# Hybrid encoder layer: token forms one iteration sooner, additions that free a PSUM bank first, final norms in two interleaved parts

## The chip, the cores and the metric

The kernel runs on one core of one Trainium2 chip, in one launch. The metric is the device time of one execution in microseconds (us), lower is better; the time before is the median of three runs. The profile is of one execution, and all times of day in it are counted from the start of its span.

## The reference

One encoder layer over 1024 tokens of width 1024, in float32, then a final norm:

```python
h = h + hybrid_mixer(rms_norm(h, ln_mix_g), ...)      # RG-LRU group and attention group, then y @ w_o
h = h + conv_glu_ffn(rms_norm(h, ln_ffn_g), w_up, conv_w, conv_b, w_down)
return rms_norm(h, final_norm_g)

def rms_norm(x, g):
    return x * lax.rsqrt(mean(x * x, axis=-1) + 1e-6) * g
def conv_glu_ffn(xn, w_up, w, b, w_down):
    u = depthwise_conv(xn @ w_up, w, b, 1)            # three taps along the tokens
    g, val = u[..., :2816], u[..., 2816:]
    return (silu(g) * val) @ w_down
```

## The kernel before, in words

Everything is float32, and each matrix product is made of three TensorE passes: an operand is split into a high part (ScalarE writes the copy rounded to fp32r) and a low part (VectorE or GpSimd subtracts the high part from the source), and high x high, high x low and low x high are added up in one PSUM bank. `split` (lines 57 to 67) does that; line 62 is its ScalarE copy, line 67 its subtraction.

After the attention the rest of the program is in hand-written order: inside `manual_schedule` each engine and the DMA queue (SP) execute in the order of the program text. `order.close()` ends one such block and the next one begins; at that seam the build's planner merges the two orders, so that a few instructions of the second block can stand before the last ones of the first. A pool's PSUM bank or SBUF slot that is given out again makes its next writer wait until all its readers are done.

The output projection is a loop over the 8 token tiles `i` (128 tokens each). Iteration `i` transposes the attention half of tile `i+1` (`mla_in`), multiplies (`mix`, 24 matmuls), adds to `hh[i]`, stores `hh[i]` to DRAM (`hs`), turns an earlier tile's normalised rows into the token forms that the next stage needs (`tr2`: four transposes per form, then a split), and normalises `hh[i]` in place (`norm2`, line 937 its last multiplication). The four banks of `oneC` go round: each transposed or projected block takes the next one.

The feed-forward products use a two-level scheme with seven products for eight (Strassen-Winograd): forms B11, B21, B22 and the sums T1 to T4 of the token side (`sums_a`, `sums_b` lines 953 to 961, `tr_sum`), and for each of the 22 column pairs `j` four forms of the up-projection weights (`W[0..3, j]`, made by `combine`, lines 972 to 977, and `split`). `prod(n, j, ps, new)` is 12 matmuls into one bank. `spare` hands out, in turn, banks that the pair loop doesn't use yet, for the transposes of the forms; the order in which forms take spare banks decides which bank waits for which split.

The pair loop (line 1321 on) runs seven products for pair `j`, and beside them on ScalarE and VectorE: the convolution taps of the gate (`glu_gate`) and of the value (`glu_value`, with the Silu of line 1192) of this and the pair before, the product of the two (`glu_out`, which spills the seven forms for the down projection to DRAM), the weight forms of pair `j+1` (`prep0`, `prep_sums`), and the additions between products (`add`, line 1083). One of them, `add(vh, vl, ts_)`, reads the bank `vl` that product 4 then writes on, so product 4 waits for it. In the last pair, `look_ahead` fetches and makes the first operands of the down projection.

The down projection is a loop over `todo`: 7 passes `p` of 11 blocks `q`, 12 matmuls each, in four banks `x` or `y`. `make(n)` builds a block's operands four blocks ahead: it splits a spilled form (`A` part) and a form of the down weights (`W` part); for some passes VectorE first forms a sum of weights. The last four blocks of pass 6 stand apart (`LAST`), ordered by token tile: all four blocks of tile `j`, then the addition to `hh[4+j]`, then its final norm. `norm3` squares a row tile on ScalarE with a running sum, takes the root, gets the reciprocal root on VectorE in five [128,1] operations (lines 83 to 87), multiplies by the gain (line 1276) and stores. In pass 6 the norms of tiles 0 to 3 stand between the makes.

## Time and profile before

| | us |
|---|---|
| median of 3 runs (lowest, highest) | 1245.88 (1244.98, 1251.24) |
| the profiled execution | 1245.23 |
| its span, first to last instruction | 1243.3 |
| TensorE matmul busy | 1174.3 (94%) |
| TensorE weight load busy | 974.5 (78%) |
| VectorE busy | 939.1 (76%) |
| ScalarE busy | 642.8 (52%) |
| GpSimd busy | 268.2 (22%) |
| mean granted TensorE clock | 0.977 |

The span is the time from the first to the last instruction of the profiled execution; 1.93 us of the execution lie outside it. PE is TensorE (PEld its weight loads), DVE VectorE, ACT ScalarE, POOL GpSimd, SP the queue that issues DMAs. The profile divides the chain of work that ended last as 77% PE, 14% DVE, 4% issue, 3% ACT and 2% DMA. A timeline row is start, duration, engine, line, operation, output<-inputs, shapes and count; in brackets stand the idle time of the engine before it and what ended that.

### The profile page before, as it was taken

To read this page: it belongs to the slowest core of one execution; us is meant where nothing else is said; L and a number is where in the kernel's file an instruction comes from. 1 tells how busy PE (TensorE), PEld (TensorE's weight loads), DVE (VectorE), ACT (ScalarE), POOL (GpSimd) and SP (SyncE) were. 2 spreads that over 40 slices of the span, in tenths; PEclk is the share of its full clock that TensorE was granted. 3 is DMA by queue.
4 is the path that set the end of the run, shared out by engine and by line. 5 is a ranking of instruction groups with operands and counts; after the bars stand their busy time and mean duration, and the time that the engine had idled before them with its cause. 6 is when DMAs were issued, how large, how long until landed. Compare 5 with 4: busy or idle time off the path is not lost.

```text
span 1243.3 us, 15331 instructions
## 1 busy us (share of the span) xinstructions
PE 1174.3 (94%) x5668; PEld 974.5 (78%) x5668; DVE 939.1 (76%) x1374; ACT 642.8 (52%) x1029; POOL 268.2 (22%) x150
## 2 busy tenths in 40 slices
PE   6998887999999999998799999999999989999994
PEld 5976765788888888787688888888888878888873
DVE  6788789777777755586778787787877867787675
ACT  5645466676777763343544445444454445344442
POOL 2224456631212433353101011010110000000000
PEclk9999998999999999999899999999999999999997
DMA  6311110000000142230333322333223179653222
GB/s 210 101 43 43 34 35 17 18 1 1 1 1 1 51 154 85 85 111 8 93 110 103 122 96 79 108 104 122 91 84 108 53 258 348 207 178 105 98 94 84
DMA packets 93578, 113.37 MB, mean 91 GB/s; under 512 B 5184, under 2 KB 59840, under 8 KB 93504
## 3 DMA queue, kind: packets, MB, share of 16 engines
q1 hardware_dynamic: 93504, 112.40, 27.3%
q8 instruction: 44, 0.72, 0.2%
q14 instruction: 30, 0.25, 0.1%
HBM read 82.76 MB, written 28.57 MB: 90 GB/s over the span
## 4 chain that ended last, share of the span: by engine, by line
PE 77%; DVE 14%; issue 4%; ACT 3%; DMA 2%; SPq 0%; POOL 0%; DVEq 0%; ACTq 0%; POOLq 0%
PE vl L1080 18%; PE x L1269 7%; PE y L1269 7%; PE pt L763 4%; PE p L1080 4%; PE gh L1080 4%; PE gl L1080 4%; PE av L774 3%; PE av L773 3%; PE sc L70 2%; PE sc L71 2%; PE sc L72 2%; DVE bc L223 1%; PE pso L71 1%; PE pso L72 1%
## 5 line engine op out<-in xcount | busy, mean ns | idle before, releaser
L1080 PE MATMUL vl<-T,w 128*128 128x512 f32 x792 | 198.7, 400 | 10.1 <-DVE vh L1083 10.1
L1080 PEld LDWEIGHTS vl<-T,w 128*128 128x128 f32 x792 | 150.7, 191 | 46.9 <-DVE vh L1083 11.3
L67 POOL TENSOR_TENSOR w<-rg,w 128x1024 fp32r<-128x1024 f32 x21 | 52.0, 2478 | 356.8 <-ACT w L62 220.2
L749 DVE TENSOR_REDUCE nm<-sc 128x1 f32<-128x1024 f32 x64 | 78.2, 1221 | 30.3 <-PE sc L72 30.0
L62 ACT ACTIVATE ptb<-pt 128x512 fp32r<-128x512 f32 x128 | 70.2, 596 | 58.7 <-PE pt L763 57.6
L67 DVE TENSOR_TENSOR ptb<-pt,ptb 128x512 fp32r<-128x512 f32 x128 | 82.9, 680 | 7.0 <-ACT ptb L62 7.0
L756 ACT ACTIVATE pr<-sc,nm 128x1024 f32<-128x1024 f32 x64 | 71.7, 1120 | 2.3 <-DVE nm L749 2.3
L763 PE MATMUL pt<-ident,pr 128*128 128x128 f32 x512 | 67.6, 274 | 3.3 <-DVE ptb L67 3.3
L763 PEld LDWEIGHTS pt<-ident,pr 128*128 128x128 f32 x512 | 59.3, 140 | 14.1 <-DVE ptb L67 5.4
L773 PE MATMUL av<-ptb,vt 128*128 128x256 f32 x256 | 66.1, 295 | 0.0
L1173 ACT ACTIVATE c<-gh,vv 128x512 f32<-128x512 f32 x22 | 17.1, 779 | 92.0 <-DVE gh L1083 92.0
L1080 PE MATMUL gh<-B,w 128*128 128x512 f32 x264 | 64.3, 392 | 0.0
L774 PE MATMUL av<-ptb,vt 128*128 128x256 f32 x256 | 63.9, 286 | 0.0
L1080 PE MATMUL p<-T,w 128*128 128x512 f32 x252 | 62.5, 397 | 0.0
L1269 PE MATMUL x<-abS 128*128 128x512 f32 x264 | 60.2, 389 | 0.0
L1269 PE MATMUL y<-abS 128*128 128x512 f32 x264 | 60.2, 389 | 0.0
L1080 PEld LDWEIGHTS gh<-B,w 128*128 128x128 f32 x264 | 49.5, 188 | 11.4
L1080 PE MATMUL vl<-B,w 128*128 128x512 f32 x240 | 58.4, 392 | 0.0
L1080 PE MATMUL gl<-B,w 128*128 128x512 f32 x240 | 57.6, 389 | 0.0
L1269 PEld LDWEIGHTS x<-abS 128*128 128x128 f32 x264 | 49.6, 188 | 10.3
L1269 PEld LDWEIGHTS y<-abS 128*128 128x128 f32 x264 | 49.6, 188 | 10.3
L1080 PEld LDWEIGHTS p<-T,w 128*128 128x128 f32 x252 | 47.4, 188 | 11.4
(638 smaller groups left out, 2979.9 us busy)
## 6 DMA issues: line engine op xcount, KB each, us to landing
rg<-in_wup SPq DMA_DIRECT2D x22, 512.0 KB, 4.1
rv<-in_wup SPq DMA_DIRECT2D x22, 512.0 KB, 3.8
S<-c SPq DMA_DIRECT2D x44, 256.0 KB, 2.6
wr<-in_wdn SPq DMA_DIRECT2D x44, 256.0 KB, 5.4
stS<-S SPq DMA_DIRECT2D x44, 256.0 KB, 2.9
A<-c SPq DMA_DIRECT2D x33, 256.0 KB, 2.1
stA<-A SPq DMA_DIRECT2D x33, 256.0 KB, 5.2
wost<-in_wo SPq DMA_DIRECT2D x8, 512.0 KB, 3.7
```

Source lines behind the costliest of these rows:

```text
L62: act.activation(hi, src, AF.Copy)
L67: (dve if lo_on == "dve" else pool).tensor_tensor(out=lo, in0=src, in1=hi.bitcast(F32), op=ALU.subtract)
L70: pe.matmul(ps, l[0], r[0], start=start, stop=False)
L71: pe.matmul(ps, l[0], r[1], start=False, stop=False)
L72: pe.matmul(ps, l[1], r[0], start=False, stop=stop)
L749: dve.reduce_max(nm[t], sc[t], axis=AX, negate=True)
L756: act.activation(pr[t], sc[t], AF.Exp, bias=nm[t], accum_out=rowsum[:, h, i:i + 1])
L763: pe.transpose(pt[:, ts(c, P)], pr[t][:, ts(4 * kh + c, P)], ident)
L773: pe.matmul(av[:, 0:256], lv, ptb[buf][:, 0, c, :], start=(c == 0), stop=False)
L774: pe.matmul(av[:, 0:256], lv, ptb[buf][:, 1, c, :], start=False, stop=(c == NT - 1))
L1080: pe.matmul(ps, w[:, l, ko + k, :], b[:, r, k, :], start=a_, stop=z_, skip_group_check=True)
L1269: pe.matmul(ps, ab[:, 0, l, ts(j, P)], ab[:, 1, r, :], start=a_, stop=z_, skip_group_check=True)
```

## The change

The token forms of tile `i-1`, and not `i-2`, are made in iteration `i` of the output projection, and the sums with them; the sums of tile 7 go from GpSimd to VectorE and stand between the first form transposes, of which T2 comes first. The sums of pair 1's weights are formed in the scratch `c0`, earlier. In pairs 0, 1 and the last, the addition that product 4 waits for stands before (last pair: between) the operand work that it followed, and the first weight form of pair 2 and the first two fetches of the down operands move to the start of an iteration. In the down projection a sum of weights (b21 + b11) is formed one pass sooner. The squares of the right half of tiles 4 to 7 are summed during pass 6, and in the last four tiles the VectorE part of a norm stands one tile later than its ScalarE part.

```diff
         for i in range(NT):
...
-            if i >= 2:
-                tr2(i - 2, oneC)
+            if i >= 1:
+                tr2(i - 1, oneC)
             norm2(i)
-            if i >= 6:
-                sums_b(i - 2, pool)
+            if i >= 5:
+                sums_b(i - 1, pool)
             if 4 <= i < NT - 1:
                 sums_a(i, pool)
...
-        tr2(6, spare)
-        sums_b(6, pool)
-        sums_a(7, pool)
...
     c0 = stp.tile([P, S], F32, tag="st", name="c0")
+    tr_sum("T2", 0, spare)
     prod(1, 0, VL[0], True)
-    tr_sum("T2", 0, spare)
+    sums_a(7, dve)
     tr_sum("T2", 1, spare)
+    tr_sum("T2", 2, spare)
+    split(W[0, 1][:, 0], W[0, 1][:, 1], raw[1][0], "act", "dve")
     copy(c0[:, lo], VL[0])
-    split(W[0, 1][:, 0], W[0, 1][:, 1], raw[1][0], "act", "dve")
     prod(2, 0, GL, True)
-    tr_sum("T2", 2, spare)
     tr2(7, spare)
-    sums_b(7, pool)
+    sums_b(7, dve)
     add(GL, GL, c0[:, lo])
     spares.remove(S1)
     prod(1, 1, VL[1], True)
     tr_sum("T2", 3, spare)
+    s3 = c0[:, lo].rearrange("p (k n) -> p k n", k=4)
+    combine(1, s3, dve)
     prod(2, 1, S1, True)
...
-    def prep_sums(j, between=None, zs=(3, 2, 1)):
+    def prep_sums(j, between=None, zs=(3, 2, 1), s3=None):
         rg, rv = raw[j]
-        s3 = fw.tile([P, 4, P], F32, tag="s3", name=f"s3{j}")
-        combine(j, s3, dve)
+        if s3 is None:
+            s3 = fw.tile([P, 4, P], F32, tag="s3", name=f"s3{j}")
+            combine(j, s3, dve)
...
-        if bf == "T4":
-            dve.tensor_tensor(out=b21, in0=b21, in1=b11, op=ALU.add)
         split(ab[:, 1, 0], ab[:, 1, 1], src, "act", "dve")
         if bf == "B21":
             dve.tensor_tensor(out=b11, in0=b12, in1=b11, op=ALU.subtract)
+        if bf == "B22":
+            dve.tensor_tensor(out=b21, in0=b21, in1=b11, op=ALU.add)
...
-    def norm3(i):
-        junk = fw.tile([P, D], F32, tag="w3", bufs=2, name=f"jf{i}")
-        act.activation(junk, hh[i], AF.Square, accum_out=ss_f[:, i:i + 1])
-        r = rsqrt(ss_f[:, i:i + 1], 1, 1.0 / D, f"rf{i}")
+    def norm3_half(i):
+        junk = fw.tile([P, 512], F32, tag="w3", bufs=2, name=f"jg{i}")
+        act.activation(junk, hh[i][:, hi], AF.Square, accum_out=ss_f[:, i:i + 1])
+        for k, m in ((0, 1.0), (1, -0.5)):
+            dve.tensor_scalar(out=part[:, k, i:i + 1], in0=ss_f[:, i:i + 1], scalar1=m / D, scalar2=m * EPS, op0=ALU.mult, op1=ALU.add)
+
+    def norm3_act(i, part_only=False):
+        junk = fw.tile([P, 512 if part_only else D], F32, tag="w3", bufs=2, name=f"jf{i}")
+        act.activation(junk, hh[i][:, lo] if part_only else hh[i], AF.Square, accum_out=ss_f[:, i:i + 1])
+        return rsqrt_act(ss_f[:, i:i + 1], 1, 1.0 / D, f"rf{i}", part[:, 0, i:i + 1] if part_only else None)
+
+    def norm3_dve(i, sq, part_only=False):
+        r = rsqrt_dve(sq, ss_f[:, i:i + 1], 1, 1.0 / D, f"rf{i}", part[:, 1, i:i + 1] if part_only else -0.5 * EPS)
...
     fetch_raw(2, 0)
     prod(7, 0, VL[0], False)
-    prep_sums(1, None, (2, 1, 3))
     ts_ = aside(T1, 0)
     add(VH[0], VL[0], ts_)
     prod(3, 0, GH, True)
+    gh = GH
+
+    def first_gh():
+        add(gh, gh, c0[:, hi])
+        add(gh, gh, ts_)
+
+    prep_sums(1, None, (1, 2), s3)
+    first_gh()
+    split(W[3, 1][:, 0], W[3, 1][:, 1], s3, "act", "dve")
     cgs[0] = conv_start(0, GL)
-    add(GH, GH, c0[:, hi])
-    add(GH, GH, ts_)
     prod(4, 0, VL[0], False)
...
-        if 1 < j < NPAIR - 1:
+        if j < NPAIR - 1:
             prep0(j + 1)
+        else:
+            fetch_to(2)
...
-        if j == 1:
-            prep0(2)
-        else:
+        if j > 1:
             prod(2, j, C11[j], False)
...
         prod(7, j, vl, False)
-        if not last:
+        if j == 1:
+            add(vh, vl, ts_)
+            prep_sums(2)
+        elif not last:
             prep_sums(j + 1, lambda: add(vh, vl, ts_))
         else:
-            look_ahead()
+            fetch_to(8)
+            make(0)
+            make(1)
             add(vh, vl, ts_)
+            make(2)
+            make(3)
...
+    part = f2.tile([P, 2, NT], F32, name="part")
...
         if p == 6 and q < 4:
-            norm3(q)
+            norm3_dve(q, norm3_act(q))
+            norm3_half(4 + q)
+    sqs = {}
     for j in range(4):
         for q in range(NQ - LAST, NQ):
             down(xs[j], j, ready[len(todo) - NQ + q], False, q == NQ - 1)
         into(1, 0, xs, j)
-        norm3(4 + j)
+        sqs[j] = norm3_act(4 + j, True)
+        if j:
+            norm3_dve(3 + j, sqs[j - 1], True)
+    norm3_dve(7, sqs[3], True)
```

## Rows read from the trace of the kernel before

**Rows 1.** Who waited for whom, PE alone: us in total, times, longest us.
```profile
PE vl L1080 <- DVE vh L1083: 10.1, 3, 4.2
PE x L1269 <- ACT res L62: 6.1, 4, 3.9
```
**Rows 2.** Busy time by stretch; after the engines PEclk, DMA share, GB/s.
```profile
614.00:982.00 368.00, 367.97 (x1584) 298.71 (x1585) 292.57 (x381) 174.33 (x228) 46.29 (x19) 1.00 0.32 103
596.80:600.20 3.40, 3.40 (x10) 2.63 (x9) 2.52 (x4) 0.78 (x1) 0.00 (x0) 0.50 0.97 278
613.90:617.30 3.40, 3.27 (x8) 2.60 (x9) 2.55 (x4) 1.56 (x2) 0.00 (x0) 0.50 0.64 186
1008.00:1012.00 4.00, 4.00 (x17) 3.28 (x18) 3.93 (x7) 1.99 (x4) 0.00 (x0) 1.00 0.62 230
```
**Rows 3.** Timeline of PE, forms and first pairs, in order.
```profile
567.84 2.38 PE L1080 MATMUL vl<-B,wo 128*128 128x512 f32 x9 [2.33 <-DVE wo L67]
...
580.34 3.06 PE L1080 MATMUL t<-T,w 128*128 128x512 f32 x12 [0.70 <-DVE T L67]
...
595.93 7.35 PE L1080 MATMUL vl<-T,w 128*128 128x512 f32 x24 [4.25 <-DVE vh L1083]
...
614.03 4.54 PE L1080 MATMUL vl<-T,w 128*128 128x512 f32 x12 [2.38 <-DVE vh L1083]
...
623.97 2.24 PE L1080 MATMUL vl<-T,w 128*128 128x512 f32 x9
```
**Rows 4.** Timelines of DVE and POOL at the end of the projection.
```profile
552.85 1.10 DVE L85 TENSOR_TENSOR rh6t<-rh6r 128x1 f32<-128x1 f32 x1
...
562.04 2.29 DVE L937 SCALAR_TENSOR_TENSOR h<-h,rh7r,g 128x1024 f32<-128x1024 f32 x1
...
566.04 1.74 DVE L67 TENSOR_TENSOR wo<-rg,wo 128x1024 fp32r<-128x1024 f32 x1
...
552.62 1.31 POOL L960 TENSOR_TENSOR h<-h,h 128x512 f32<-128x512 f32 x1
```
**Rows 5.** Groups by line and shape, 586 to 640 us.
```profile
L67 DVE TENSOR_TENSOR w<-rv,w 128x1024 fp32r<-128x1024 f32 x3 | 3.7, 1217 | 0.0
...
L1192 ACT ACTIVATE c<-c 128x1024 f32<-128x1024 f32 x3 | 3.2, 1061 | 0.3 <-DVE c L1178 0.3
...
L1173 ACT ACTIVATE c<-gh,vv 128x512 f32<-128x512 f32 x3 | 2.3, 778 | 8.4 <-DVE gh L1083 8.4
...
L1178 DVE SCALAR_TENSOR_TENSOR c<-gh,vv,c 128x512 f32<-128x512 f32 x3 | 2.3, 751 | 0.1
...
L976 DVE TENSOR_TENSOR rg<-rv,rg 128x512 f32<-128x512 f32 x3 | 2.1, 692 | 2.7 <-POOL w L67 2.5
```
**Rows 6.** Timelines of PE and DVE, last pair.
```profile
1008.00 3.06 PE L1080 MATMUL vl<-T,w 128*128 128x512 f32 x12 [3.46 <-DVE vh L1083]
...
1002.55 0.69 DVE L67 TENSOR_TENSOR abA<-wr,abA 128x512 fp32r<-128x512 f32 x1
```
**Rows 7.** Timelines of PE and DVE, last pass and tail.
```profile
1190.44 19.20 PE L1269 MATMUL x<-abA 128*128 128x512 f32 x84
...
1203.20 0.68 DVE L67 TENSOR_TENSOR abA<-stA,abA 128x512 fp32r<-128x512 f32 x1
...
1206.23 0.15 DVE L83 TENSOR_SCALAR rf2xh<-ss_f 128x1 f32<-128x1 f32 x1 [0.35 <-ACT jf L1273]
...
1207.34 1.28 DVE L1276 SCALAR_TENSOR_TENSOR hf<-hf,rf2r,g 128x1024 f32<-128x1024 f32 x1
1208.54 0.68 DVE L67 TENSOR_TENSOR res<-stA,res 128x512 fp32r<-128x512 f32 x1
...
1227.25 0.68 DVE L1083 TENSOR_TENSOR hf<-x,hf 128x512 f32<-128x512 f32 x1
...
1231.46 0.68 DVE L1083 TENSOR_TENSOR hf<-x,hf 128x512 f32<-128x512 f32 x1
...
1238.67 1.42 DVE L1276 SCALAR_TENSOR_TENSOR hf<-hf,rf7r,g 128x512 f32<-128x512 f32 x2
```

More of the change, by code (lines that the diff above doesn't have):

```diff
@@ L1301, in make @@
             ready[n] = operands(*ORDER[p], q, home)
-    def look_ahead():
-        fetch_to(6)
-        for n in range(4):
-            make(n)
     fetch_raw(2, 0)
     prod(7, 0, VL[0], False)
-    prep_sums(1, None, (2, 1, 3))
     ts_ = aside(T1, 0)
```

## The prediction

> **What bounds the kernel now.** I read the waits of PE first, then busy time by stretch, then the timelines where PE stands still. From 614 to 982 us PE is busy 367.97 of 368 us at a granted clock of 1.00 [rows 2]: nothing that this change does to ScalarE, VectorE or the queues can shorten that stretch. What can be won lies where PE waits. Of those waits two kinds are touched here: 10.1 us in three waits for the addition that frees the bank `vl`, and 6.1 us for the split operands `res` of the last pass [rows 1]. The reader should see that the three bank waits are 4.25, 2.38 and 3.46 us [rows 3, 6], and that two of them cost more than themselves: after 595.93 and after 614.03 there are 3.4 us at a granted clock of 0.50, that is 1.2 instead of 2.4 GHz [rows 2], where 1.7 us of work each is lost. After the 3.46 us wait the clock stayed at 1.00 [rows 2]. The third place is the tail, where no engine is busy: the additions of two neighbouring row tiles start 4.21 us apart (1231.46 less 1227.25), and the last multiplication ends at 1238.67 + 1.42 = 1240.1 [rows 7].
>
> **The own time.** The sum is made against the profiled execution, 1245.23 us, of which 1243.3 are span; the median of the runs is 0.65 higher, less than I can resolve, so no correction is made.
>
> **Part one, the tail and the last pass.** Before, each block of pass 6 with a norm behind it takes 1208.54 - 1203.20 = 5.34 us on VectorE [rows 7], since it goes low part, sum of weights, ScalarE copy, low part, norm, one after the other. The sum of weights goes to the pass before, where VectorE then has three operations of 0.7 us for 12 matmuls of PE (2.7 us), so it is hidden there; without that cover it would cost 11 x 0.7 = 7.7 us. The new step has two low parts of 0.68, five small operations that last at most 1207.34 - 1206.23 = 1.11, the multiplication with 1.20 to the next start, and two new [128,1] operations. These are not in the trace; between 0.15 (a small one) and 0.35 more for a wait as before the same row, I take 0.2 each [rows 7]. Sum 4.07; overlapped starts take some 0.15 off: 3.9. PE begins pass 6 at 1190.44 and passes 84 matmuls in 19.2 us, 0.227 each [rows 7]. VectorE is done with the `y` additions 0.9 later, at 1191.3, so the last of the seven remaining blocks is ready at 1191.3 + 4 x 3.9 + 3 x 1.3 = 1210.8. PE wants it after 93 matmuls, at 1211.5. So PE doesn't stop; the margin is 0.7, and the point from which it stops is a step of 4.1 us.
>
> The half squares are new on ScalarE: 512 columns with a running sum, between a 512-column copy with scale (0.78) and a 1024-column one (1.06) [rows 5]; I take 0.8 with its read-out. ScalarE's step is then two copies, a whole square, a root and a half square, about 3.2 us, under VectorE's 3.9, so it is hidden; if not, it has 0.7 to go.
>
> Row tile 4 is then complete at 1190.44 + 96 x 0.227 + 0.2 = 1212.4, tile 7 at 1220.6. VectorE's order is add 4, add 5, norm 4, add 6, norm 5, add 7, norm 6, norm 7; a norm is five small operations back to back (1.0) and 1.2, and its root was taken on ScalarE meanwhile. Add 5 starts at 1215.2 (12 matmuls after tile 4): 0.7 and 2.2 give 1218.1; add 6 and norm 5, 2.85, give 1220.9; add 7 and norm 6 give 1223.75; norm 7 has 1.0 and two halves of together 1.42 and ends at 1226.2. Against 1240.1 that is **13.9 us less**; what follows, the last stores, is the same. The price ends are 8.8 (PE stops as today, see the second rival) and 14.6 (every small operation at 0.15).
>
> **Part two, the last pair.** PE is ready for product 4 at 1008.00 - 3.46 = 1004.54. VectorE's second block, the last work now ahead of the addition, ended at 1002.55 + 0.69 = 1003.24 even with the fetches as late as they were [rows 6]; the addition takes 0.7, so it is done at 1003.95 and nothing waits. The two blocks that go behind it are wanted by PE 5 us and more later. The early fetches stand in SP's queue ahead of one spill and wait for the slot of form B11, which product 1 of this pair lets go; all else in the queue has its old order. **3.4 us less**; at worst the fetch order costs the same again (0).
>
> **Part three, forms and first pairs.** I follow them to one point, product 6 of pair 2, which started at 623.97 [rows 3] and after which PE doesn't wait.
>
> In the projection loop the number of form transposes stays; tile `i-1` is normalised before PE ends the multiplication of tile `i`, so they find their rows ready. At its end VectorE sets the pace. Row 552.85 shows a [128,1] product that took 1.10 us while a GpSimd sum ran from 552.62 on for 1.31, and the multiplication of tile 7 took 2.29 where the same shape takes 1.28 at rest [rows 4, 7]: such operations wait for GpSimd's. The two sums taken from GpSimd let the last multiplication run at rest (1.0 less) and the split of pair 1's weights take 1.22 instead of 1.74 [rows 4, 5]; the same two pairs of sums cost VectorE 4 x 0.69 [rows 5], half of it ahead of that split. With 0.4 us from PE's four transposes that left the loop's end, product 1 of pair 1 starts 0.5 sooner than 567.84. Against that, one form fewer takes a spare bank, so all later forms move on by one, and the bank that product 5 wants (0.70 wait at 580.34 [rows 3]) is freed one split of 0.6 later. The four operations of `combine` (2.8 us) move into VectorE's gaps there. Net 0, between 1.8 sooner (a row tile's whole contention) and 1.7 later.
>
> The Trainium skill, "SBUF — State Buffer", section "Who interferes with whom", has it that a VectorE instruction with two SBUF inputs and a GpSimd instruction that reads SBUF exclude each other for a whole instruction. By that rule the sums that the change pulls forward keep GpSimd busy under the last two norms, which speaks against a gain here; without it the tile would be ready 1.8 sooner. The contended row agrees with the rule, and I go by it.
>
> Product 3 of pair 0 ended at 595.93 - 4.25 = 591.7 [rows 3] and now ends at 592.0. From there two chains race. PE: products 4 | 6, 5, 7, 3, 4 of pair 1 | 1, 5 of pair 2, eight of 2.77 = 22.2. VectorE, from the addition to `VH` at 589.2 on: 0.7, two weight splits 2.4, two additions 1.3, a split 0.6, a wait of 0.25 on ScalarE's tap (0.78), eight taps of 0.75, the gate product 1.2: 601.7, where it waits for product 7 of pair 1. PE's product 7 itself waits 0.2 for the copy behind the Silu and ends at 592.0 + 4 x 2.77 + 0.2 = 603.3. Then addition 0.65, `combine` 2.8, three splits 3.1, addition 0.7, ScalarE's tap 0.85, four taps 3.0: 614.4; the Silu 1.06 and a copy 0.6: 616.1 [rows 5]. PE arrives at product 6 at 592.0 + 22.2 + 0.2 = 614.4 and waits 1.7. So the 10 us of waits and slow clock (4.25 + 2.38 + 3.4) become one new wait of 1.7: 623.97 - 616.1 = 7.9 less. The first weight form of pair 2 now stands ahead of the value's taps on ScalarE; its copy needs columns whose fetch waits in SP for a slot that the first of the two weight splits frees, at 591.1. The value's taps on VectorE begin at 597.6, behind a copy (1.06) and a tap (0.78), so the fetch has 4.7 us to land; each us more holds up taps, Silu and product 7 by one. At the seam of the two blocks the planner may put the last form's transposes behind product 7; its bank is then what product 3 waits for, 0.8 later. I take **7.2 us less**, with 3.7 and 9.6 as ends.
>
> **Sum.** 13.9 + 3.4 + 7.2 = 24.5; 1245.23 - 24.5 = 1220.7.
>
> **The rivals.**
> First: the first pairs give it back. PE now waits about 3 us ahead of product 1 of pair 1 (it arrives sooner, the split hardly) and 1.7 ahead of product 6. A 2.38 us wait was followed by the half clock and 3.46 was not [rows 2, 3, 6], so either may cost 1.7. Both, and the seam's 0.8: 7.2 becomes 3.0, time 1224.9. The Trainium skill, "TensorE: Matmul & The Clock Gate", section "HAM oscillation — how this bites in real kernels", has gaps between matmul groups send the clock to half so that the next group starts cold; by that rule alone this rival would be the rule, and the trace bears it out in two of the three bank waits.
> Second: the operand chain stays the bound of pass 6. If the step stays 5.34, the last block is ready at 1191.3 + 21.4 + 3.9 = 1216.6, 5.1 late: time 1225.8. For it: 5.34 is what is measured. Against: two of its links are gone by the text.
> Third: the additions don't come sooner, because merging at the seam or a fetch that blocks SP holds VectorE up as before. Then only the tail remains, 1245.23 - 13.9 = 1231.3. For it: three queues meet there. Against: order inside a block is that of the text.
> Fourth, slower: in the attention only PE's order is written by hand; the rest is the planner's, over 59 steps. If it orders VectorE otherwise and a step loses over 24.5 / 59 = 0.42 us, the gain is gone; at 0.6 the time is 1256. Against: nothing changes ahead of the projection loop.
>
> **How the numbers follow.** Forecast 0.66 (own range 1217.5 to 1223.5), first rival 0.16, second 0.07, third 0.04, fourth 0.04, better than 1217 (no new wait, all upper ends) 0.03. The range of 1217 to 1228 leaves out the last three of these, 0.11, and the far edges of the others. A change of 0.5%, 6.2 us, is what a measurement of this kernel tells from none; faster by more than that are all cases but the fourth (part of it is the same): faster 0.95, same 0.02, slower 0.03.
>
> **What would show it.** PE without a wait for `vh` at all; no idle PE in pass 6 and a clock of 1.00 to its end; row additions in the tail 2.85 apart; the last multiplication ending 14 us after tile 4's last matmul; one wait near product 6 of pair 2 of about 1.7 us. It is wrong if PE waits on `res`, if half-clock stretches follow 567 or 614, or if the stretch to 500 us has another length.

## The result, and the profile after

The changed kernel takes 1227.36 us (median of 4 runs, 1227.13 to 1228.26), the kernel before 1247.36 beside it (4 runs, 1244.98 to 1251.24): a ratio of 0.9838 [0.981, 0.9866], 20 us faster (17 to 24). The forecast was 1220.7, range 1217 to 1228; the time lies in the range by 0.6 us, and above the 1217.5 to 1223.5 that the forecast gave as its own. The profiled execution took 1227.5 us with a span of 1225.7; the comparison below is made between the two spans, 1243.3 and 1225.7.

Who waited for whom, PE alone, after: us in total, times, longest. The three waits for the bank `vl` and those for `res` [rows 1] are gone; what stands there now are waits for split forms, weights and normalised rows.

```profile
PE pshB L942 <- DVE h L937: 3.8, 3, 1.6
...
PE vl L1076 <- DVE wo L67: 2.6, 1, 2.6
PE vl L1076 <- ACT gl L1082: 1.5, 1, 1.5
PE gh L1076 <- DVE T L67: 1.4, 1, 1.4
PE t L1076 <- DVE T L67: 1.3, 1, 1.3
```

Timeline of PE after, in order of time: where these waits fall. The first three are in the projection loop, where PE transposes a tile that has just been normalised; the rest answer to [rows 3], and the last two lines to the head of [rows 7].

```profile
525.21 1.17 PE L942 MATMUL pshB<-ident,h 128*128 128x128 f32 x8 [1.58 <-DVE h L937]
...
553.67 0.63 PE L942 MATMUL pshB<-ident,h 128*128 128x128 f32 x4 [0.88 <-DVE h L937]
...
561.27 0.65 PE L942 MATMUL pshB<-ident,h 128*128 128x128 f32 x4 [1.36 <-DVE h L937]
...
572.35 3.85 PE L1076 MATMUL vl<-B,wo 128*128 128x512 f32 x10 [2.58 <-DVE wo L67]
576.70 3.05 PE L1076 MATMUL s<-B,wo 128*128 128x512 f32 x12
...
586.86 3.06 PE L1076 MATMUL t<-T,w 128*128 128x512 f32 x12 [1.29 <-DVE T L67]
...
596.91 3.02 PE L1076 MATMUL gh<-B,w 128*128 128x512 f32 x12 [1.41 <-DVE T L67]
...
624.50 1.88 PE L1076 MATMUL vl<-T,w 128*128 128x512 f32 x7 [1.50 <-ACT gl L1082]
...
1187.38 18.98 PE L1269 MATMUL x<-abA 128*128 128x512 f32 x83
...
1206.42 11.04 PE L1269 MATMUL x<-res 128*128 128x512 f32 x48
```

Busy time by stretch, after (columns as in [rows 2]): one stretch at the half clock is left in this part, behind the wait at 572.35; the last pass runs at full clock to its end.

```profile
573.50:576.90 3.40, 3.40 (x12) 2.71 (x11) 1.30 (x2) 0.00 (x0) 0.00 (x0) 0.53 0.02 5
614.00:982.00 368.00, 366.50 (x1584) 297.23 (x1583) 294.86 (x385) 176.38 (x231) 46.24 (x19) 1.00 0.32 103
1187.00:1217.50 30.50, 30.46 (x135) 24.89 (x133) 23.62 (x64) 17.76 (x42) 0.00 (x0) 1.00 0.25 95
```

To see where the time went I cut each profile at five points of PE's timeline, the same instructions in every kernel. A runs from the first transposes of the projection's second loop (`psyt`, tile 0) to the start of product 2 of pair 1 (into `s`); B from there to product 3 of pair 0 (into `gh`); C to product 6 of pair 2 (the point of part three); "rest" to the start of the last pass; D to the end of the span. All are differences of start times in the profiled executions, us:

| kernel | run median | psyt at | A | B | C | A+B+C | rest | D |
|---|---|---|---|---|---|---|---|---|
| before | 1247.36 | 502.32 | 68.46 | 17.88 | 35.31 | 121.65 | 566.47 | 52.86 |
| after | 1227.36 | 503.91 | 72.79 | 20.21 | 27.59 | 120.59 | 562.88 | 38.32 |
| tail_only | 1235.86 | 504.98 | 69.48 | 18.33 | 36.59 | 124.40 | 569.42 | 38.30 |
| forms_back | 1224.92 | 503.90 | 70.71 | 17.96 | 29.46 | 118.13 | 562.90 | 38.37 |
| one_turn_on | 1225.84 | 504.72 | 71.00 | 17.96 | 28.62 | 117.58 | 562.90 | 38.30 |
| pairs_back | 1229.28 | 504.27 | 72.10 | 20.70 | 30.60 | 123.40 | 562.79 | 38.34 |
| norms_whole | 1230.91 | 503.53 | 71.24 | 20.21 | 27.83 | 119.28 | 562.86 | 42.23 |
| t4_late | 1239.32 | 502.73 | 71.21 | 20.21 | 27.79 | 119.21 | 562.89 | 51.17 |
| copy_first | 1223.00 | 503.95 | 71.47 | 17.96 | 26.74 | 116.17 | 564.40 | 38.28 |
| sums_late | 1223.01 | 502.38 | 70.38 | 17.96 | 28.66 | 117.00 | 562.89 | 38.33 |
| copy_first2 | 1223.74 | 503.05 | 69.81 | 17.98 | 25.17 | 112.96 | 564.32 | 38.27 |
| w01_first | 1224.18 | 504.08 | 68.67 | 20.19 | 28.20 | 117.06 | 562.86 | 38.30 |
| combined | 1221.64 | 504.59 | 69.99 | 17.94 | 25.16 | 113.09 | 564.20 | 38.32 |
| three_moves | 1221.05 | 505.35 | 66.98 | 19.75 | 25.16 | 111.89 | 564.19 | 38.27 |

Before to after: 14.5 from D, 3.6 from "rest", 1.1 from A to C, and 1.6 lost ahead of `psyt`: 17.6, the difference of the spans. Code ahead of `psyt` is the same in all fourteen kernels, and its start lies anywhere from 502.3 to 505.4; so I compare kernels by A to D and "rest", which leave that out, and by the medians. The four kernels with 564.2 to 564.4 in "rest" have a wait of 1.15 to 1.28 us there, at product 4 of pair 2.

### The profile page after: what moved, and what is told of

The parts are those of the page before. It is cut to its first block, busy times and chain, and to the rows that moved or that the text cites. A ratio compares the mean times of both kernels' runs of the same rounds, so it can differ in the third digit from the quotient of the medians.

```text
span 1225.7 us, 15357 instructions
## 1 busy us (share of the span) xinstructions
PE 1167.1 (95%) x5668; PEld 970.8 (79%) x5668; DVE 939.6 (77%) x1386; ACT 641.3 (52%) x1037; POOL 260.2 (21%) x146
## 4 chain that ended last, share of the span: by engine, by line
PE 81%; DVE 12%; ACT 2%; DMA 2%; issue 2%; SPq 0%; DVEq 0%; POOL 0%; ACTq 0%
PE vl L1076 19%; PE x L1269 9%; PE y L1269 7%; PE gh L1076 5%; PE gl L1076 4%; PE pt L763 4%; PE p L1076 4%; PE av L774 3%; PE av L773 2%; PE sc L70 2%; PE sc L71 2%; PE sc L72 2%; DVE bc L223 1%; PE pso L71 1%; PE pso L72 1%
## 5 line engine op out<-in xcount | busy, mean ns | idle before, releaser
L1076 PE MATMUL vl<-T,w 128*128 128x512 f32 x792 | 195.7, 396 | 2.0 <-ACT gl L1082 1.5
L773 PE MATMUL av<-ptb,vt 128*128 128x256 f32 x256 | 64.9, 292 | 0.0
L774 PE MATMUL av<-ptb,vt 128*128 128x256 f32 x256 | 62.6, 283 | 0.0
```

The lines of the kernel that those rows point to most:

```text
L773: pe.matmul(av[:, 0:256], lv, ptb[buf][:, 0, c, :], start=(c == 0), stop=False)
L774: pe.matmul(av[:, 0:256], lv, ptb[buf][:, 1, c, :], start=False, stop=(c == NT - 1))
L1076: pe.matmul(ps, w[:, l, ko + k, :], b[:, r, k, :], start=a_, stop=z_, skip_group_check=True)
```

## The experiments

The theory after this profile was this. Tail and last pair did what was forecast; the forecast's gain at the forms was lost in three places: the projection loop, where PE now stands ahead of rows that are not normalised; the half clock behind the wait at 572.35; and the rotation of the spare banks. The rival was the forecast's first one: that the first pairs themselves gave it back.

**The tail alone (tail_only).** The kernel before with the moved sum, the halved and interleaved norms, and nothing else of the change.

> The kernel before with only the changes of the down projection and the final norms. Theory: this part is worth what the changed kernel shows between the start of the last pass and the end (38.3 us for 52.9), 14.5 us whatever the rest does: 1232.5 to 1233.5 on a before of 1247.4, ratio 0.988 to 0.989. Rival: part of it is bought by the earlier parts (operands fetched earlier in the last pair), then it is worth under 12 us here, a time over 1235.

Measured: 1235.86 (4 runs, 1232.23 to 1238.90), ratio 0.9908 [0.988, 0.9936]. D is 38.30, that of the whole change, so the tail's 14.5 us are its own. The rest is not quite the kernel before: in the profile the three bank waits are there, and each was followed by the half clock. Timeline of PE, that kernel, the second and the third:

```profile
619.37 4.61 PE L1080 MATMUL vl<-T,w 128*128 128x512 f32 x12 [2.38 <-DVE vh L1083]
...
1014.01 5.39 PE L1080 MATMUL vl<-T,w 128*128 128x512 f32 x12 [4.06 <-DVE vh L1083]
```

The reader should see 4.61 and 5.39 us for twelve matmuls that take 3.06 in [rows 6]. With that, and four runs that lie 7 us apart, its median is above what was expected: 11.6 us below the kernel before that ran beside it (1247.43), which by its number is the rival's case. The sections say otherwise: D gained the 14.5, while A to C and "rest" lost 2.8 and 3.0 in this profile, taken on the slowest of the four runs.

**The norms in one piece (norms_whole).**

```diff
-            norm3_dve(q, norm3_act(q))
-            norm3_half(4 + q)
+            norm3(q)
...
-        sqs[j] = norm3_act(4 + j, True)
-        if j:
-            norm3_dve(3 + j, sqs[j - 1], True)
-    norm3_dve(7, sqs[3], True)
+        norm3(4 + j)
```

> The changed kernel with each tail norm back in one piece (one square over 1024 columns, its VectorE part straight behind it); the moved sum of the seventh form stays. Theory: the four row additions of the tail go back from 2.72 to 4.2 us apart, three gaps of 1.5, and the last square takes 1.06 instead of 0.62, so last pass to end grows from 38.3 to about 43.2 and the time from 1227.4 to about 1232.3. Rival, that the norms had slack and the whole 14.5 of the tail came from the operand chain: 38.3 and 1227.4 stay.

Measured: 1230.91 (1229.69 to 1232.17), D 42.23. The theory's place was right, its size 1 us too large: the additions are 4.22 us apart as it said, but the last norm then has VectorE to itself, where in the changed kernel it queues behind the norm of tile 6. Timeline of DVE, two neighbouring row additions of that kernel:

```profile
1207.63 0.69 DVE L1079 TENSOR_TENSOR hf<-x,hf 128x512 f32<-128x512 f32 x1 [4.49 <-PE x L1269]
...
1211.85 0.68 DVE L1079 TENSOR_TENSOR hf<-x,hf 128x512 f32<-128x512 f32 x1
```

**The sum back in the last pass (t4_late).**

```diff
+        if bf == "T4":
+            dve.tensor_tensor(out=b21, in0=b21, in1=b11, op=ALU.add)
         split(ab[:, 1, 0], ab[:, 1, 1], src, "act", "dve")
...
-        if bf == "B22":
-            dve.tensor_tensor(out=b21, in0=b21, in1=b11, op=ALU.add)
```

> The changed kernel with the sum for the seventh form back in the last pass, between the two splits of each operand; the halved, interleaved norms stay. Theory: VectorE's step for one operand grows from 3.36 to about 4.75 while norms run beside it and from 1.20 to 2.6 for the last three, so the last operand is split about 10 us later, some 7 us after PE wants it; PE waits for res, last pass to end grows from 38.3 to about 45, the time to about 1234.4. Rival, that the sum fits in VectorE's idle time as it does in the pass before: no wait for res, 1227.4.

Measured: 1239.32 (1237.86 to 1240.63), D 51.17: 12.9 us more, not 7. Timeline of PE at the end of that kernel's last pass:

```profile
1205.29 0.49 PE L1269 MATMUL x<-res 128*128 128x512 f32 x1 [1.26 <-ACT res L62]
...
1210.75 1.95 PE L1269 MATMUL x<-res 128*128 128x512 f32 x3 [4.00 <-ACT res L62]
1213.34 1.95 PE L1269 MATMUL x<-res 128*128 128x512 f32 x3 [0.65 <-ACT res L62]
1215.93 11.89 PE L1269 MATMUL x<-res 128*128 128x512 f32 x39 [0.64 <-ACT res L62]
```

The waits for `res` add up to 6.8 us with a short one of 0.23 between, as expected; what the expectation left out is the clock: it was granted at 0.50 from within the second wait on, so that the remaining matmuls took longer as well (39 in 11.89 us, against 48 in 11.04 after). Busy time by stretch, this kernel:

```profile
1207.90:1221.60 13.70, 9.56 (x19) 5.75 (x20) 7.31 (x13) 3.95 (x8) 0.00 (x0) 0.50 0.10 38
```

Norms and sum taken back singly cost 3.9 and 12.9, together more than the 14.5 they brought. That late operands and slow norms hide behind each other would explain it; this was not followed further.

**The old order of forms (forms_back).** The changed kernel with the projection loop's transposes and sums where they were.

```diff
-            if i >= 1:
-                tr2(i - 1, oneC)
+            if i >= 2:
+                tr2(i - 2, oneC)
...
-            if i >= 5:
-                sums_b(i - 1, pool)
+            if i >= 6:
+                sums_b(i - 2, pool)
...
+        tr2(6, spare)
+        sums_b(6, pool)
```

T2's form of tile 2 goes behind product 2 of pair 0 again; the sums of tile 7 stay on VectorE.

> The changed kernel with the token forms made two iterations later again, their sums on GpSimd at their old places, and T2's third tile behind product 2; all else as changed. Theory A (the forms now follow a norm that is not ready, held up by a store and by GpSimd's sums): PE's waits of 1.58, 0.88 and 1.36 us in the projection loop go, the stretch from the first psyt transposes to product 6 of pair 2 shrinks from 120.6 to 116.5 to 118 us, the time from 1227.4 to 1223.5 to 1225. Rival B (VectorE's chain through the first pairs is the bound, whatever the forms do): the stretch stays at 120 to 121 us, the time within 0.8 us of the changed kernel.

Measured: 1224.92 (1222.74 to 1226.55), 0.982 [0.9798, 0.9841]. A is 70.71, 2.1 less than after, although PE waits 3.13 us for the same weights and the half clock follows; B is 17.96 instead of 20.21. PE's waits for a normalised tile shrink to 0.23; one of 1.74 at tile 1 stays, in another form (below). As the change stands, the part that gives it its name, forms one iteration sooner, does not pay by these sections: without it the stretch is 2.5 us shorter at product 6 of pair 2 (118.13, just past the expected 116.5 to 118, against 120.59). But this run also takes back the rotation of the banks, which is the next experiment and accounts for the 2.25 in B. With the rotation alone put right and the forms sooner, the stretch is 117.58, in a profile in which the half clock (1.8 us) did not come. So whether sooner forms pay in themselves is not shown, nor whether late ones would still be better with the corrections below. The medians can't say either: the two intervals overlap.

**One turn of the banks (one_turn_on).**

```diff
-        turn, spares = [0], [VH[0], VH[1], GH, T1, S1]
+        turn, spares = [1], [VH[0], VH[1], GH, T1, S1]
```

> The changed kernel with the round of spare banks started one turn later, so that every form has the bank of before. PE's wait ahead of product 5 of pair 0 falls from 1.29 to 0.7 and the 1.41 us ahead of product 3 go in both theories. Theory A (each wait of PE costs itself): the stretch from psyt to product 6 of pair 2 shrinks by 1.5 to 2.0 us. Theory B (from the last form's split on it is VectorE's chain that counts): by no more than 0.8, since product 6 of pair 2 then waits longer than 1.5 us.

Measured: 1225.84 (1223.21 to 1227.17), 0.9826 [0.9807, 0.9845]. In all kernels with the old assignment of banks B is 17.9 to 18.3, in those with the new one 20.2 to 20.7 (three_moves has the old one; its B holds another wait, below). So one form fewer ahead of the rotation, and nothing else, costs 2.25 us: product 5 of pair 0 and product 3 of pair 0 wait 0.70 and 0 instead of 1.29 and 1.41, because the last T4 form no longer sits in the bank that product 3 wants. Timeline of PE, this kernel, and its addition to `VH` in pair 0 on DVE:

```profile
572.92 2.61 PE L1076 MATMUL vl<-B,wo 128*128 128x512 f32 x10 [2.59 <-DVE wo L67]
...
593.68 2.99 PE L1076 MATMUL gh<-B,w 128*128 128x512 f32 x12
...
606.59 3.06 PE L1076 MATMUL vl<-T,w 128*128 128x512 f32 x12 [1.53 <-ACT gh L1082]
...
622.30 3.04 PE L1076 MATMUL vl<-T,w 128*128 128x512 f32 x12 [1.52 <-ACT gl L1082]
...
595.39 0.70 DVE L1079 TENSOR_TENSOR vh<-vl,ts 128x512 f32<-128x512 f32 x1
```

One microsecond of it is given back in C (28.62 against 27.59): PE comes sooner to product 7 of pair 1 and waits there for ScalarE. The first line shows something else: the same wait of 2.6 us as at 572.35 after, and no half clock behind it (2.61 us for ten matmuls, not 3.85). That is 1.8 of the 3.0 us by which the stretch to product 6 of pair 2 is shorter; the edit's own share is 1.2, between what theory A and theory B gave it.

**The first pairs as they were (pairs_back).** The changed kernel with the additions that free the banks and pair 2's first weight form in their old places, in pairs 0 and 1; the part for pair 1:

```diff
-        if j == 1:
-            add(vh, vl, ts_)
-            prep_sums(2)
-        elif not last:
+        if not last:
             prep_sums(j + 1, lambda: add(vh, vl, ts_))
```

> The changed kernel with the order of pairs 0 and 1 of before (weight splits ahead of the additions that free the bank; first weight form of pair 2 late), all else as changed. If the additions are worth what their waits were in the kernel before, with the half clock behind them, 4.25 + 2.38 + 3.4 less the new waits of 2.0: 6 to 8.5 us slower, 1233.5 to 1236. If the early part's small gain (1.1 us for 7.2) comes from these additions doing little: within 3 us of the changed kernel.

Measured: 1229.28 (1226.46 to 1230.57), 0.9853 [0.9834, 0.9872]; C is 30.60, 3.0 more than after, and a bank wait is back in each of the two pairs, the second with the half clock behind it. Timeline of PE:

```profile
600.89 5.83 PE L1076 MATMUL vl<-T,w 128*128 128x512 f32 x24 [0.81 <-DVE vh L1079]
...
617.68 4.61 PE L1076 MATMUL vl<-T,w 128*128 128x512 f32 x12 [2.58 <-DVE vh L1079]
```

The 6 to 8.5 us of the expectation did not come: the median is 1.9 us above the changed kernel's, with intervals that overlap, which is inside the 3 us of the other case. So of the 7.7 us that the change took out of C, the place of the additions and of pair 2's first weight form accounts for 3.0. The wait of 4.25 in pair 0 is 0.81 here even in the old order: three of the four operations of `combine` (2.1 us) no longer stand between the last form's split and the addition, and PE comes 1.4 later, held at product 3 by the bank. Neither was taken back singly. That the first pairs give the gain back is not the main cause even so: C is 27.59 where 27.1 was forecast (below).

**The first weight split sooner (w01_first).** One line of the changed kernel goes up, ahead of the T2 forms:

```diff
+    split(W[0, 1][:, 0], W[0, 1][:, 1], raw[1][0], "act", "dve")
     tr_sum("T2", 0, spare)
     prod(1, 0, VL[0], True)
     sums_a(7, dve)
     tr_sum("T2", 1, spare)
     tr_sum("T2", 2, spare)
-    split(W[0, 1][:, 0], W[0, 1][:, 1], raw[1][0], "act", "dve")
```

> The changed kernel with one step moved: the split of pair 1's first weight form stands ahead of the three T2 forms on ScalarE and VectorE, not behind them. Theory that PE's wait of 2.58 us for it and the half clock behind it are a part of what the forecast missed: both go, the second part of product 1 of pair 1 comes at 65.9 us after psyt instead of 68.4, product 2 of pair 1 about 4 us sooner, and 1 to 3 us of it are left at product 6 of pair 2 (120.6 to 117.6 to 119.6), so 1224.4 to 1226.4. Rival, that the splits of the T forms are then 1.2 to 2.3 us later and PE waits for them instead: 1227.4.

Measured: 1224.18 (1223.16 to 1226.08), 0.9801 [0.9777, 0.9824]. Product 6 of pair 2 comes at 117.06, 3.5 sooner. Timeline of PE:

```profile
567.85 3.04 PE L1076 MATMUL vl<-B,wo 128*128 128x512 f32 x12
...
572.34 0.66 PE L942 MATMUL vh<-ident,h 128*128 128x128 f32 x4 [1.44 <-DVE h L960]
```

Product 1 of pair 1 runs through; a new wait of 1.44 stands behind it, for the sums of tile 7, which now come after the split. A fell by 4.1, of which 1.3 are not the edit's: the wait at tile 1 was 0.31 here and 1.58 in the profile of after (last section). The other 2.8 are, to a tenth, the wait of 2.58 and 1.8 of half clock, less the new 1.44. So by the sections the place of this one split was worth nearly 3 us to the changed kernel; 2.33 of that wait stood in the kernel before as well [rows 3].

**GpSimd's sums late (sums_late),** on one_turn_on: `sums_b(i - 2, pool)` from iteration 6 on and the last pair of sums after the loop, with the forms still one iteration sooner.

> The variant with the bank rotation one turn on, and GpSimd's second sums back where they were (one iteration later), the token forms still one iteration sooner. Theory that GpSimd's sums slow VectorE's norms of tiles 5 and 6 (1.1 to 1.2 us for operations that take 0.16 alone, 2.2 for one that takes 1.28): the waits of 0.88 and 1.36 us for the norm in the projection go, the second part of product 1 of pair 1 comes 1.5 to 2 us sooner after psyt (66.4 instead of 68.2), of which 0 to 1.5 is left at product 6 of pair 2 (117.6 to 116.1). Rival, that those norms are late for the store of their rows: the waits stay, 68.2 and 1225.8.

Measured: 1223.01 (1221.62 to 1223.78), 0.9804 [0.9781, 0.9827]; in the profile the second part of product 1 of pair 1 comes at 67.6, between the two expectations, and product 6 of pair 2 only 0.6 sooner (117.00). The median is lower by more, 2.8; 2.3 of that stand in this profile ahead of `psyt`. Both theories miss. The first has the mechanism: the wait of 0.88 is gone and the norm of tile 5 takes 1.28 at rest (tile 6 still has sums beside it: 2.20, and a wait of 0.70). But the sums then run beside tile 7's norm too, and PE waits 1.91 for one of the last two. First DVE (the norm), then PE, this kernel:

```profile
548.46 1.28 DVE L937 SCALAR_TENSOR_TENSOR h<-h,rh5r,g 128x1024 f32<-128x1024 f32 x1
```

```profile
564.11 0.66 PE L942 MATMUL s<-ident,h 128*128 128x128 f32 x4 [1.91 <-POOL h L960]
```

**Copies ahead of the Silu (copy_first, copy_first2),** on one_turn_on. In pairs 1 and 2 ScalarE's copy of the bank that PE wants next is put ahead of the Silu; copy_first also moves the split of pair 2's first weight form behind it, copy_first2 does not.

```diff
-        glu_value(j - 1, vl_, vh_)
+        glu_taps(j - 1, vl_, vh_)
+        if j > 2:
+            glu_silu(j - 1)
...
             copy(GH, vl)
+        if j <= 2:
+            glu_silu(j - 1)
         ts_ = aside(t, j)
```

> The variant with the bank rotation one turn on, and in pairs 1 and 2 ScalarE's copy of the bank that PE waits for put ahead of the Silu and of the split of pair 2's first weight form. Theory that ScalarE's queue holds PE there: the waits of 1.53 and 1.52 us at product 7 of pair 1 and product 6 of pair 2 go, psyt to product 6 of pair 2 falls from 117.6 to about 114.7, and the time from 1225.8 to about 1223. Rival, that VectorE's taps hold both engines: PE waits as long for a bank that VectorE reads, 117.6 and 1225.8 stay.

Measured: 1223.00 (1219.99 to 1224.64), 0.9802 [0.9776, 0.9828]. The wait at product 7 of pair 1 went, the one at product 6 of pair 2 stayed (1.41), and a new one of 1.28 came behind product 6, so that product 1 of pair 3 lies 42.2 us behind product 3 of pair 0, against 42.6 without the edit. The median is where it was expected and the reason given for it did not hold. The sections do not show that gain: the 1.4 us by which product 6 of pair 2 comes sooner (116.17 against 117.58) are lost again in "rest" (564.40 against 562.90), and the two intervals overlap. Timelines of DVE and POOL, this kernel:

```profile
608.28 2.48 DVE L974 TENSOR_TENSOR s<-rg,rv 128x512 f32<-128x512 f32 x1
...
607.81 2.39 POOL L67 TENSOR_TENSOR w<-rg,w 128x1024 fp32r<-128x1024 f32 x1 [42.38 <-ACT w L62]
```

The moved split put GpSimd's half of it beside the first operation of `combine`, which took 2.48 us instead of 0.68. That was the next thing to take away.

> As copy_first, but the split of pair 2's first weight form stays where the change has it, so that GpSimd's half of it runs beside VectorE's taps (which read PSUM) and not beside its combination of the weights. Theory that copy_first lost its gain to that neighbour (one combination of 0.68 took 2.48 us): all combinations take 0.7, and from product 3 of pair 0 to product 1 of pair 3 it is about 39.7 us, against 42.6 with the rotation alone and 42.2 in copy_first; the time is 1.5 to 3 us below the rotation alone. Rival, that the taps themselves hold PE: about 42.

Measured: 1223.74 (1220.46 to 1225.24), 0.9791 [0.9768, 0.9814]. C is 25.17, eight products of 2.77 and one of 3.0: PE doesn't wait any more between product 3 of pair 0 and product 6 of pair 2. Behind that point it does. Timeline of PE:

```profile
616.01 2.94 PE L1076 MATMUL vl<-T,w 128*128 128x512 f32 x12
...
628.50 1.67 PE L1076 MATMUL vl<-T,w 128*128 128x512 f32 x6 [1.27 <-DVE vh L1079]
```

Product 4 of pair 2 meets its bank's addition, still between two weight splits there, as in all pairs but the first two and the last. So from product 3 of pair 0 to product 1 of pair 3 it is 40.57, not 39.7; neither theory has it exactly, the first is nearer. The medians of copy_first and copy_first2 do not differ.

**All corrections (combined).** Rotation, late sums, T2's third form behind product 2, weight split first, copies first with the split as in copy_first2.

> All corrections in one: rotation one turn on, GpSimd's second sums at their old places, T2's third form behind product 2, pair 1's first weight split ahead of the T2 forms, bank copies ahead of Silu in pairs 1 and 2. Theory that the waits of the forms and first pairs are separate: no wait over 1 us between psyt and pair 3, product 6 of pair 2 at about 113.5 us after psyt (the forecast had 114.5), the time about 1218 to 1221. Rival, that VectorE's work from the last T4 split on sets the end of the stretch whatever is moved ahead of it: about 117 and 1223.

Measured: 1221.64 (1220.26 to 1222.06), 0.9776 [0.9757, 0.9794]: faster than the kernel before and, since the interval lies wholly below that of the changed kernel, than that too. Product 6 of pair 2 comes at 113.09, as expected; that no wait over 1 us is left is wrong (1.55 at tile 1, 1.03 for the weight split, 1.72 for the sums of tile 7, 1.18 at product 4 of pair 2). The weight split, now first, ran beside GpSimd's late sums. Timeline of DVE:

```profile
567.50 2.30 DVE L67 TENSOR_TENSOR wo<-rg,wo 128x1024 fp32r<-128x1024 f32 x1
```

**The sums as the change has them (three_moves).** Rotation, weight split first, copies first, and T2's last form behind product 2 of pair 1; GpSimd's sums stay pulled forward.

> The changed kernel with its sums on GpSimd left where the change put them and four moves: rotation one turn on, pair 1's first weight split ahead of the T2 forms, T2's last form behind product 2 of pair 1, bank copies ahead of Silu in pairs 1 and 2. Theory that the sums pulled forward pay once the first weight split is out of the way (VectorE's last norm and that split run alone, 1.3 and 1.2 us, where GpSimd's late sums stretch them to 2.3 each): product 2 of pair 1 starts about 68.3 us after psyt instead of 70.0 in the kernel with all corrections, product 6 of pair 2 at 111 to 112, the time 1218 to 1221. Rival, that the sums' place makes no difference once the rest is mended: 113 and 1221.6.

Measured: 1221.05 (1220.50 to 1223.75), 0.9784 [0.9766, 0.9803]. Product 2 of pair 1 starts at 66.98, sooner than expected, product 6 of pair 2 at 111.89, as expected. But the rival has the better case: A and B together differ from combined by 1.20 us, and 1.24 of that is the wait at tile 1, 0.31 here and 1.55 there. What the moved form took away in A (its wait for tile 7's sums, 1.72 before, 0.26 now) came back in B, where product 6 of pair 0 waits 1.05 for that form. The two times can't be told apart either.

## Why the prediction was right, and the step that failed

The time fell in the range because the tail and the last pair brought what was forecast, with a little to spare, and because the range was wide enough for a rival; the sum itself was 6.7 us too low, 6.1 of them in part three. That the number came to lie 0.6 us inside the upper edge is luck.

**Tail and last pass: right.** 13.9 forecast, 14.5 measured. PE does not stop in the last pass and has the full clock to its end, as said. Timeline of DVE after, two successive blocks, then row additions and the last multiplication:

```profile
1191.55 0.68 DVE L67 TENSOR_TENSOR abA<-stA,abA 128x512 fp32r<-128x512 f32 x1
...
1194.91 0.68 DVE L67 TENSOR_TENSOR abA<-stA,abA 128x512 fp32r<-128x512 f32 x1
...
1214.78 0.69 DVE L1079 TENSOR_TENSOR hf<-x,hf 128x512 f32<-128x512 f32 x1
...
1217.50 0.69 DVE L1079 TENSOR_TENSOR hf<-x,hf 128x512 f32<-128x512 f32 x1
...
1221.09 1.41 DVE L1285 SCALAR_TENSOR_TENSOR hf<-hf,rf7r,g 128x512 f32<-128x512 f32 x2
```

The step is 3.36 us where 3.9 was forecast: the small operations stood nearer to their lower bound. The additions come 2.72 apart (2.85 forecast), the pace of PE's twelve matmuls, so the tail is now bound by PE and not by VectorE up to the last addition. The second rival (operands still late) is out; t4_late shows that its 1225.8 and the forecast's 7.7 for a sum that is not hidden were both too low: 12.9, of which 6.8 are waits and most of the rest the half clock that came with them.

**Last pair: right.** 3.4 forecast, 3.6 measured in "rest"; product 4 starts without a wait.

**Forms and first pairs: one half about right, the other wrong.** 7.2 forecast, 1.1 measured. The race of PE against VectorE and ScalarE in the first pairs (C) was forecast as 27.1 us (product 3 takes 3.0 to its end at 592.0; PE is at product 6 at 616.1) and took 27.59, against 35.31 before; the new wait at product 6 of pair 2 was forecast as 1.7 and is 1.50. Part of that agreement is luck. The forecast had the addition to `VH` 0.2 us behind the start of product 3 (589.2, and 592.0 less 3.0). In one_turn_on, where nothing holds product 3, it starts 1.7 behind (595.39 against 593.68), because the last T4 split stands ahead of it, and C is 28.62. In the changed kernel the bank holds product 3 for 1.41, which gives VectorE that time; the cost stands in B. This is the case that the forecast put at the seam, at 0.8, and behind which it went from 7.9 to 7.2. Timeline of PE after, the last form's transposes, behind product 7 and in `gh`, the bank of product 3 at 596.91:

```profile
594.90 0.60 PE L942 MATMUL gh<-ident,h 128*128 128x128 f32 x4
```

In the kernel before they stood behind product 7 as well (588.31), but in `vh`.

The step that failed lies ahead of it: tile `i-1` "is normalised before PE ends the multiplication of tile `i`, so they find their rows ready", and with it "Net 0, between 1.8 sooner and 1.7 later". A and B together grew by 6.7 us, where 0.3 was forecast, or 1.0 with what was taken off for the seam. Timelines of DVE and POOL after, the norms of tiles 1, 5, 6 and 7 and what GpSimd did:

```profile
522.85 2.21 DVE L937 SCALAR_TENSOR_TENSOR h<-h,rh1r,g 128x1024 f32<-128x1024 f32 x1 [2.78 <-DMA hs<-h]
...
549.88 1.21 DVE L86 TENSOR_TENSOR rh5u<-rh5t,rh5xh 128x1 f32<-128x1 f32 x1
...
551.32 2.20 DVE L937 SCALAR_TENSOR_TENSOR h<-h,rh5r,g 128x1024 f32<-128x1024 f32 x1
...
559.01 2.20 DVE L937 SCALAR_TENSOR_TENSOR h<-h,rh6r,g 128x1024 f32<-128x1024 f32 x1
...
566.75 1.28 DVE L937 SCALAR_TENSOR_TENSOR h<-h,rh7r,g 128x1024 f32<-128x1024 f32 x1
...
549.79 1.29 POOL L960 TENSOR_TENSOR h<-h,h 128x512 f32<-128x512 f32 x1
551.15 1.29 POOL L961 TENSOR_TENSOR h<-h,h 128x512 f32<-128x512 f32 x1
```

Timelines of PE and DVE before, tile 1:

```profile
522.67 0.66 PE L942 MATMUL pshB<-ident,h 128*128 128x128 f32 x4 [1.76 <-DVE yl L67]
...
519.04 2.97 DVE L937 SCALAR_TENSOR_TENSOR h<-h,rh1r,g 128x1024 f32<-128x1024 f32 x1 [0.76 <-DMA hs<-h]
```

Three things are to be seen. The norm works in place, so at tile 1 it waits for the store of its own rows to `hs`, and now PE stands directly behind it. That is no loss in itself: in the kernel before PE waited there too, 1.76, for a bank that the split of `yl` frees, which on VectorE stood behind the same norm. What is new are the other two waits, 0.88 and 1.36. The norms of tiles 5 and 6 run beside the sums that the change itself pulled forward, and take 2.20 instead of 1.28, one of their small operations 1.21. And the norm of tile 7 is at rest, the 1.0 that the forecast did count. The forecast quoted the Trainium skill, "SBUF — State Buffer", section "Who interferes with whom", on this exclusion and used it to cancel a gain; the trace agrees with the rule, and what was missed is that PE now stands directly behind the norms that are held up.

In numbers, A (4.3 more, where 0.5 less was forecast): the loop's waits are 3.8 instead of the one of 1.76, 2.1 more, all of it at tiles 5 and 6; the wait for the weights is 0.25 longer; the half clock behind it takes 1.8 (A of 72.79 against 71.00 in one_turn_on, whose instructions up to there are the same); 0.2 are left over. B (2.3 more): the rotation, which one_turn_on takes back whole. The forecast had the rotation, at 0.6 for product 5 (0.59 measured), and product 3 behind the seam, at 0.8, where 1.41 were.

**The first rival** (1224.9) named the half clock at this wait and at product 6, and the seam's 0.8, of which 0.7 had already been taken off the 7.9. The half clock came at the first place and not at the second, and the wait at product 3 came, so the rival had 1.8 and a part of the 1.41; the loop's 2.1 no rival had. The time, 1227.4, is 6.7 above the forecast: 6.1 at the forms and first pairs and 1.6 ahead of `psyt`, less 0.8 that tail and last pair brought beyond their share, and a tenth or two between span and run. The other rivals are out: no wait for `res` (second), the additions do come sooner (third: product 4 waits in none of the three places), and the stretch ahead of the projection is the same but for its start-up (fourth).

Two signs that the forecast named for being wrong did appear: a half-clock stretch behind 567, and another length of the stretch to 500 us. The first was a real miss; the second is spread between executions of the same code (502.3 to 505.4 in the table).

## What to carry to other kernels

Issuing work one step sooner on the engine that sets the pace gains only if its inputs are ready a step sooner too: ask what their producer itself waits for (its own store, a neighbour on another engine). Where buffers rotate, follow a shift of the ring to every later user, and price the wait at each. A wait behind which the clock may fall is priced with a range, here 2.6 to 4.4 us for the same 2.58.

## What the runs showed of the hardware that was not expected

The same wait can cost two prices. PE stood 2.57 to 2.59 us for pair 1's first weight form in seven profiles whose PE order is the same up to there; in five (after, pairs_back, norms_whole, t4_late, copy_first) the next ten matmuls took 3.40 to 4.14 us and the clock went to its lower level (0.53 in the stretch above), in two (one_turn_on, copy_first2) they took 2.61 at full clock. The kernel before (2.33, then 2.60) and tail_only (2.32, then 3.43) are such a pair too. The Trainium skill, "TensorE: Matmul & The Clock Gate", section "HAM oscillation — how this bites in real kernels", has a gap between groups of matmuls send the clock down; the gaps of its example are DMA waits of about 3 to 5 us, so for waits as short as these it does not make the half clock the rule, as the forecast had it behind its first rival. The trace shows the half clock behind 2.58 us in five of seven; what decides between five and two stays open.

The norm of tile 1 has two prices as well: 1.34 to 1.50 us in six kernels with the sooner forms (PE waits 0.31 to 0.34) and 2.06 to 2.40 in five (1.55 to 1.58), by when the store of its rows is done (DVE waits 2.24 to 2.41 and 2.58 to 2.92). The later start itself is the smaller part. In the six the norm starts 0.2 to 0.4 us ahead of GpSimd's first combination of weights (L974), which then takes 2.26; in the five that operation starts ahead of it or within 0.04 us of it and takes 1.28, and the norm takes the longer time. This is 1.3 us between runs with no cause in the code that was changed.

A VectorE operation on one column beside GpSimd's sums is held up about as long as a large one: 1.21 us at 549.88 against 0.16 for the next such operation, L87 at 551.13; the multiplication at 551.32 took 0.92 longer than at rest.
